# Seven products for eight in three quarters of the second feed-forward matrix

## The chip, the cores and the metric

The kernel runs on one core of a Trainium2 chip. The metric is the device time of one execution in microseconds, the median of several runs. The profile is one execution recorded by the hardware; its times count from the first instruction of the span.

## What is computed

One encoder block on 256 tokens of width 2048 in float32: two gated branches (a chunked gated linear attention and an order-2 Hyena convolution), their merge and output projection, a LayerNorm, a squared-ReLU feed-forward network and a second LayerNorm. The change touches the feed-forward network alone:

```python
h = _layernorm(DEEPNORM_ALPHA * h + mix, ln1_g[l], ln1_b[l])
ff = jnp.square(jax.nn.relu(h @ w_ff1[l])) @ w_ff2[l]      # 2048 -> 8192 -> 2048
h = _layernorm(DEEPNORM_ALPHA * h + ff, ln2_g[l], ln2_b[l])
```

## The kernel before

**Number format.** Every matrix operand is split in two parts: `hi`, the value cast to the matmul's 32-bit format by ScalarE (a copy, line 85), and `lo`, the rest, subtracted by VectorE (line 86, `split_hi_lo`). A product is three matmuls: hi by hi, hi by lo, lo by hi. So each weight that is loaded costs one ScalarE copy and one VectorE subtraction before TensorE can use it.

**Weights.** They come as blocks of 128 partitions by 2048 floats (1 MB), in the order in which they are used. `fetch` (line 93) loads one into one of three `raw` buffers from SyncE's queue (line 99) and splits its two halves of 1024 columns into `whi` and `wlo`, of which there are three buffers each (line 107). `next_block` (line 131) fetches the next block and hands out the oldest one waiting.

**Feed-forward.** The hidden width of 8192 is worked in four quarters of 2048. `ff1(qi)` (line 1073) takes 16 blocks of the first matrix. For a block, `channel_products` (line 140) issues 16 matmuls with 512 columns (line 146: the hi weights against the hi and lo parts of all 256 tokens) and 16 with 256 columns (line 150: the lo weights against the hi part) into one PSUM bank. `channel_sum` (line 155) then copies one half of the bank out with ScalarE (line 158) and adds the other half to it with VectorE (line 159). After two blocks VectorE squares (line 1078) and the result is split into the quarter's activations. `ff2(qi)` (line 1101) takes 16 blocks of the second matrix, four for each group of 512 output columns: `token_products` (line 194) issues for each of four 128-row tiles and each of two 128-token blocks three matmuls with 512 columns (lines 205 to 207), 24 to a block. `add_ff` (line 1089) adds the two banks of a group to the running sum `z1` (line 1094; line 1092 in the first quarter).

The order of the stages is written out: `ff1(0)`, the load of the second LayerNorm's rows, `ff1(1)`, `ff2(0)`, `ff1(2)`, `ff2(1)`, `ff1(3)`, `ff2(2)`, then `ff2(3)` with its last group handled apart so that the final LayerNorm can begin early.

**What sets the order within an engine.** Every engine executes its own instructions in order. The order is fixed when the program is built, by a planner of the framework that follows the order of the code, marked priorities (`tc.high_priority`) and its own estimate of when operands are ready; semaphores then hold an instruction until its operands and its output buffer are free. There are eight PSUM banks, four under the name `mm` and four under `sd`; in the feed-forward stage only `mm` banks are used. GpSimd does nothing in this stage.

Of the kernel before, what the change touches and what calls it, by code (L numbers as in the profile page):

```python
# [16 lines left out]
P = 128  # L17
D = 2048
# [9 lines left out]
CW = D // NCH  # L28
QT = 4
W_OUT_END = 177  # L30
OPENING = 5
PIECES = tuple((k, 1) for k in range(6)) + tuple((k, 2) for k in range(6, KT, 2))

# [9 lines left out]
def block_kernel(  # L43
# [49 lines left out]
    def fetch():  # L93
        n = fetched[0]
        if n >= stop_at[0]:
            return
        fetched[0] = n + 1
        raw = wp.tile([P, D], F32, tag="raw", bufs=3, name=f"raw{n}")
        nc.sync.dma_start(raw, wblk[n])
        parts = []  # L100
        for h in range(2):
            hi, lo = weight_half(n, h)
            split_hi_lo(hi, lo, raw[:, h * 1024:(h + 1) * 1024])
            parts.append((hi, lo))
        queue.append(parts)
# [25 lines left out]
    def next_block():  # L131
        fetch()
        return queue.popleft()
# [3 lines left out]
    def channel_psum(name):  # L137
        return psum_main(name).rearrange("p (a b) -> p a b", a=2)

    def channel_products(ps, act, half, kts, ts=FULL, opens=True):  # L140
        hi, lo = half
        at = [(kt, slice(kt % 8 * P, (kt % 8 + 1) * P)) for kt in kts]

        def high():
            for kt, js in at:
                MM(ps[:, :, ts], hi[:, js], act[:, kt, :, ts], start=(kt == 0 and opens), stop=(kt == KT - 1))  # L146

        def low():
            for kt, js in at:
                MM(ps[:, 0, ts], lo[:, js], act[:, kt, 0, ts], start=False, stop=False)  # L150

        for part in (high, low) if kts[0] == 0 else (low, high):
            part()
# [4 lines left out]
            nc.scalar.activation(low, ps[:, 1], AF.Copy, scale=scale)  # L158
            nc.vector.scalar_tensor_tensor(dst, ps[:, 0], scale, low, op0=ALU.mult, op1=ALU.add)  # L159

    def channel_pair(act, name, dst=None, scale=1.0, begun=None):
        if dst is None:
            dst = base.tile([P, 2, L], F32, tag="sum", name=f"{name}_s")
        for c in range(2):
            if begun:
                ps, parts, n = begun.pop(0)
                finish_block(ps, act, parts, n)
            else:
                ps = channel_psum(f"{name}_{c}")
                parts = next_block()  # L170
                for h in range(2):
                    channel_products(ps, act, parts[h], range(8 * h, 8 * h + 8))
            channel_sum(dst[:, c], ps, f"{name}_l{c}", scale)
            pump()
        return dst

    def high_by_tokens(ps, act, half, kts, ts):
        for kt in kts:
# [55 lines left out]
    def act_tile(pool, tag, name):  # L234
        return pool.tile([P, KT, 2, L], F32R, tag=tag, name=name)
# [679 lines left out]

    tc.keep_in_program_order(nc.scalar.preload_act_table_set("natural_log_exp_and_others"))

    def resident(slots):
        parts = []
        for hi, lo in slots:  # L920
# [4 lines left out]
            for h in range(2):  # L925
                cs = slice(h * 1024, (h + 1) * 1024)
                split_hi_lo(hi[:, cs], lo[:, cs], raw[:, cs])
            parts.append([(hi[:, 0:1024], lo[:, 0:1024]), (hi[:, 1024:], lo[:, 1024:])])
        return parts

    def halves(pool, tag, name):
        t = pool.tile([P, 4, D], F32R, tag=tag, name=name)
# [100 lines left out]
            turn(at, n)  # L1033


    fts = {}

    def begin_three():
        blocks = [queue.popleft(), [], []]
        hx, lx = (ep.tile([P, D], F32R, tag=t, name=f"{t}_f") for t in ("xh", "xl"))  # L1040
# [29 lines left out]
        fetch()  # L1070
        return begun

    def ff1(qi):
        begun = begin_three() if qi == 0 else []
        f = act_tile(ep, "f", f"f{qi}") if qi % 2 == 0 else act_tile(base, "xT", f"f{qi}")
        for c2 in range(8):
            r = channel_pair(hT, f"f{qi}_{c2}", begun=begun)
            sq = nc.vector.scalar_tensor_tensor(r, r, 0.0, r, op0=ALU.max, op1=ALU.mult)
            s = slice(2 * c2, 2 * c2 + 2)
            split_hi_lo(f[:, s, 0], f[:, s, 1], r)  # L1080
            if qi == 0 and 2 <= c2 < 6:
# [3 lines left out]
        fts[qi] = f  # L1085

    st2 = ep.tile([P, NT, 8, 6], F32, tag="bst", bufs=2, name="bst2")

    def add_ff(ps, tb, at, n, qi, last=False):
        zc = z1[:, tb, at:at + n]  # L1090
        if qi == 0:
            nc.vector.scalar_tensor_tensor(zc, zc, ALPHA, ps, op0=ALU.mult, op1=ALU.add)
        else:
            nc.vector.tensor_tensor(zc, zc, ps, op=ALU.add)
        if qi == QT - 1:
            for i in range(n // 256):
                nc.vector.bn_stats(st2[:, tb, at // 256 + i, :], zc[:, i * 256:(i + 1) * 256])
            if not last:
                nc.vector.tensor_tensor(zc, zc, rows2[:, 0, at:at + n], op=ALU.mult)

    def ff2(qi, groups=4):
        for g in range(groups):
            pss = token_group(fts[qi], f"w2_{qi}{g}")
            for tb in range(NT):
                add_ff(pss[tb], tb, g * 512, 512, qi)
# [10 lines left out]
    ff2(3, 3)  # L1116
    parts = resident(halves(ep, "f", "wr2") + halves(ep, "hT", "wr3"))
    minus = ep.tile([P, P], F32, tag="minus", name="minus")
    nc.vector.tensor_scalar(minus, ident, -1.0, None, op0=ALU.mult)
    unit = ep.tile([P, P], F32R, tag="unit", name="unit")  # L1120
    nc.scalar.copy(unit, ident)
    zg = tuple(ep.tile([P, D], F32R, tag=t, name=f"{t}_z") for t in ("xh", "xl"))
    for at in (0, 768):
        split_hi_lo(zg[0][:, at:at + 768], zg[1][:, at:at + 768], z1[:, 1, at:at + 768])

    def affine(tb, at, n, rs, nb):
        zc = z1[:, tb, at:at + n]
# [8 lines left out]
    token_products([ps], fts[3], parts, [0], 0)  # L1136
    pss = [psum_main(f"w2_33_1{ch}") for ch in range(2)]
    add_ff(ps, 0, 1536, 512, 3)
# [4 lines left out]
    column_products([None, pss], fts[3], parts, [1], 0)  # L1143
    CENTRED = ((0, 512), (512, 512), (1024, 256), (1280, 256))
    po = {}
    for at, n in CENTRED[:3]:
        po[at] = psum_side(f"lo{at}")
        for part in zg:
            tc.keep_in_program_order(MM(po[at], unit, part[:, at:at + 512], start=(part is zg[0]), stop=False))
    po[1280] = po[1024][:, 256:]  # L1150
    add_ff(pss[0][:, 0:256], 1, 1536, 256, 3, last=True)
    late = z1[:, 1, 1536:2048]
    with tc.high_priority(), tc.issue_after(done.ins):
        add_ff(pss[1][:, 0:256], 1, 1792, 256, 3, last=True)
# [12 lines left out]
        nc.vector.tensor_tensor(rs, y, t, op=ALU.mult)  # L1167
# [8 lines left out]
def _layout(a):  # L1176
# [24 lines left out]
    for i in range(NCH // 2):  # L1201
# [1 line left out]
    f1 = chan(a["w_ff1"][0])  # L1203
    w2 = a["w_ff2"][0]
    f1q = [f1[16 * i:16 * (i + 1)] for i in range(QT)]
    f2q = [tok(w2[D * i:D * (i + 1)]) for i in range(QT)]
# [105 lines left out]
```

## Time and profile before

| what | value |
|---|---|
| median of 3 runs | 1826.8 us (1826.16 to 1826.92) |
| span of the profiled execution | 1826.2 us |
| TensorE busy | 1817.0 us, granted clock 1.000 |
| VectorE, ScalarE, GpSimd busy | 1286.8, 924.1 and 80.4 us |
| bytes moved | 399.55 MB, 219 GB/s in the mean |

The profiled execution's time is its span, 1826.2 us; the three runs lie within 0.7 us of it. In the views, PE is TensorE's matmuls, PEld its loads of the stationary operand, DVE is VectorE, ACT ScalarE, POOL GpSimd and SP SyncE. Matmuls are pipelined, so the duration of one (its own start to its own end) is longer than the time by which the stream advances. A row of a group gives: line, engine, operation, output and inputs with their shapes, count, then the total busy time, the mean duration in ns, and the idle time of that engine ahead of these instructions with what ended it.

### The profile page before, as it was taken

The page shows a single profiled execution, that of the slowest core. Times are in us where ns is not written, and L with a number is a line of the kernel's source. Part 1 is how long each engine was busy: PE and PEld are TensorE (multiplying, and loading weights), DVE is VectorE, ACT ScalarE, POOL GpSimd, SP SyncE. Part 2 cuts the span into 40 slices and gives each one's busy share as a digit, 9 for nine tenths or more (in the row PEclk, how much of TensorE's full clock was granted, in tenths as well). Part 3 has the DMA queues.
Part 4 walks back from the last instruction along what each step waited for, and adds up shares of the span by engine and source line. Part 5 has one row for each costly group of instructions (what it writes and reads, how often), then busy time and mean ns, then how long its engine had stood idle before and what let it go on. Part 6 is the DMA issues. An engine that isn't in the chain of part 4 may idle for free.

```text
span 1826.2 us, 22887 instructions
## 1 busy us (share of the span) xinstructions
PE 1817.0 (99%) x8931; PEld 1533.8 (84%) x8931; DVE 1286.8 (70%) x1587; ACT 924.1 (51%) x1207; POOL 80.4 (4%) x121
## 2 busy tenths in 40 slices
PE   9999999999999999999999999999999999999998
PEld 7888888888888888888888889888888888888887
DVE  6789887875689899898755567666545655565467
ACT  6678668865444444444544445444434443443332
POOL 1011110000111101020000000000000000000000
PEclk9999999999999999999999999999999999999999
DMA  8668765345788979796544763545554555555453
GB/s 326 222 257 293 253 220 204 141 162 210 235 281 255 320 249 274 259 281 230 215 186 185 288 252 137 210 185 188 193 196 186 193 195 187 195 195 187 188 197 123
DMA packets 65452, 399.55 MB, mean 219 GB/s; under 512 B 8280, under 2 KB 10856, under 8 KB 24640
## 3 DMA queue, kind: packets, MB, share of 16 engines
q1 hardware_dynamic: 47808, 336.61, 49.1%
q0 software_dynamic: 10480, 41.81, 9.9%
q10 hardware_dynamic: 7056, 19.67, 3.0%
q8 instruction: 70, 1.15, 0.2%
q14 instruction: 38, 0.31, 0.0%
HBM read 369.28 MB, written 16.25 MB: 211 GB/s over the span
## 4 chain that ended last, share of the span: by engine, by line
PE 97%; DMA 1%; DVE 1%; ACT 0%; issue 0%; SPq 0%; DVEq 0%; POOL 0%; ACTq 0%
PE f L146 12%; PE f L150 6%; PE w L205 6%; PE w L207 6%; PE w L206 6%; PE g L206 3%; PE g L205 3%; PE g L207 3%; PE ux L207 3%; PE ux L206 3%; PE ux L205 3%; PE k L146 2%; PE v L206 2%; PE v L205 2%; PE v L207 2%; PE go L206 2%
## 5 line engine op out<-in xcount | busy, mean ns | idle before, releaser
L86 DVE TENSOR_TENSOR wlo<-raw,whi 128x1024 fp32r<-128x1024 f32 x584 | 712.3, 1222 | 356.5 <-ACT whi L85 353.4
L85 ACT CAST whi<-raw 128x1024 fp32r<-128x1024 f32 x584 | 614.0, 1053 | 576.1 <-PE w L207 186.5
L146 PE MATMUL f<-hT,whi 128*128 128x512 f32 x984 | 235.1, 391 | 0.0
L146 PEld LDWEIGHTS f<-hT,whi 128*128 128x128 f32 x984 | 180.8, 188 | 35.0
L206 PE MATMUL w<-wlo,f 128*128 128x512 f32 x480 | 186.7, 389 | 0.0
L207 PE MATMUL w<-whi,f 128*128 128x512 f32 x480 | 186.7, 389 | 0.0
L205 PE MATMUL w<-whi,f 128*128 128x512 f32 x480 | 167.4, 389 | 0.0
L150 PEld LDWEIGHTS f<-hT,wlo 128*128 128x128 f32 x984 | 126.2, 191 | 4.8
L150 PE MATMUL f<-hT,wlo 128*128 128x256 f32 x984 | 127.7, 283 | 0.0
L158 ACT ACTIVATE f_l<-f 128x256 f32<-128x256 f32 x64 | 24.6, 384 | 162.2 <-PE f L146 159.3
L207 PEld LDWEIGHTS w<-whi,f 128*128 128x128 f32 x480 | 90.1, 188 | 18.8
L205 PEld LDWEIGHTS w<-whi,f 128*128 128x128 f32 x480 | 90.1, 188 | 18.7
L206 PEld LDWEIGHTS w<-wlo,f 128*128 128x128 f32 x480 | 90.1, 188 | 18.7
L159 DVE SCALAR_TENSOR_TENSOR f_s<-f,f_l 128x256 f32<-128x256 f32 x64 | 27.2, 425 | 105.0 <-ACT f_l L158 105.0
L206 PE MATMUL g<-wlo,xT 128*128 128x512 f32 x256 | 100.1, 391 | 0.0
L207 PE MATMUL ux<-whi,xT 128*128 128x512 f32 x256 | 99.9, 390 | 0.0
L207 PE MATMUL g<-whi,xT 128*128 128x512 f32 x256 | 99.8, 390 | 0.0
L206 PE MATMUL ux<-wlo,xT 128*128 128x512 f32 x256 | 99.6, 389 | 0.0
L205 PE MATMUL g<-whi,xT 128*128 128x512 f32 x256 | 93.8, 392 | 0.0
L205 PE MATMUL ux<-whi,xT 128*128 128x512 f32 x256 | 89.7, 389 | 0.0
L206 PEld LDWEIGHTS g<-wlo,xT 128*128 128x128 f32 x256 | 48.1, 188 | 10.1 <-DVE wlo L86 0.2
L206 PEld LDWEIGHTS ux<-wlo,xT 128*128 128x128 f32 x256 | 48.1, 188 | 10.1
(428 smaller groups left out, 3235.4 us busy)
## 6 DMA issues: line engine op xcount, KB each, us to landing
raw<-wblk SPq DMA_DIRECT2D x300, 1024.0 KB, 4.9
Td<-T POOLq DMA_DIRECT2D x32, 384.0 KB, 5.5
conv_sb<-conv_rows SPq DMA_DIRECT2D x12, 1024.0 KB, 11.7
Tl<-Td POOLq DMA_DIRECT2D x16, 768.0 KB, 9.1
w<-w4s ACTq DMA_DIRECT2D x16, 512.0 KB, 5.7
xw<-first SPq DMA_DIRECT2D x5, 896.0 KB, 13.4
zr<-ln_rows ACTq DMA_DIRECT2D x4, 1024.0 KB, 10.5
cx<-shift POOLq DMA_DIRECT2D x8, 508.0 KB, 8.4
```

What stands on the lines that cost most here:

```text
L85: return (nc.scalar.copy(hi, src), nc.vector.tensor_tensor(lo, src, hi.bitcast(F32), op=ALU.subtract))
L86: nc.vector.tensor_tensor(lo, src, hi.bitcast(F32), op=ALU.subtract))
L146: MM(ps[:, :, ts], hi[:, js], act[:, kt, :, ts], start=(kt == 0 and opens), stop=(kt == KT - 1))
L150: MM(ps[:, 0, ts], lo[:, js], act[:, kt, 0, ts], start=False, stop=False)
L158: nc.scalar.activation(low, ps[:, 1], AF.Copy, scale=scale)
L159: nc.vector.scalar_tensor_tensor(dst, ps[:, 0], scale, low, op0=ALU.mult, op1=ALU.add)
L205: MM(pss[tb], sh, wh, start=(kt == 0), stop=False)
L206: MM(pss[tb], sh, wl, start=False, stop=False)
L207: MM(pss[tb], sl, wh, start=False, stop=(kt == KT - 1))
```

## The change

Three of the four quarters of the second matrix are multiplied by Strassen's scheme (in the form with shared sums). Two 128-row tiles by 1024 columns of the second matrix make a 2 by 2 array of 128x512 pieces, and two token blocks by the same two tiles of the activations make a 2 by 2 array of 128x128 pieces. Instead of eight products of such pieces there are seven, each still three matmuls with 512 columns, so 21 matmuls to a block of 1 MB instead of 24. The price is sums: four sums of the weights' pieces and four of the activations' pieces before, and sums of the seven results behind.

- `fetch_sums` replaces `fetch` for the blocks of the second matrix in three quarters. It loads the block, splits the first 1024 columns and the last 512 as they are, and has **GpSimd** make four sums of 512 columns (one instruction of 1024 columns and two of 512, each reading two tiles), which ScalarE and VectorE then split as two halves of 1024. So 3584 columns of each block are split where 2048 were. The sums' tile (tag `xh`) and the tiles of the split sums (`whx`, `wlx`) exist once.
- `forms` makes the four sums of the activations on GpSimd (four instructions of 128 columns) and splits 384 and 512 columns; in the third phase, for the last quarter, which stays as it was, it splits 512 plain columns.
- `ff_phase(q)` replaces `ff2(q)` and `ff1(q + 1)`. It alternates one block of the second matrix (`forms_products`, 21 matmuls) with one of the first (32 matmuls), 16 of each. The output is worked in two groups of 1024 columns, of eight blocks each. The seven results of a group hold seven PSUM banks, so one bank is left for the first matrix.
- `take_sums` empties the seven banks after eight blocks, into `z1` or into `zacc`, which takes the place of the LayerNorm rows; four of them are ScalarE copies in the first phase, all others VectorE adds. `join_sums` makes the final sums: the first group's beside the second half of the third phase, seven on GpSimd and one on VectorE; the second group's on VectorE behind the third phase. The second LayerNorm's rows are loaded after that.
- The last quarter and the final LayerNorm do the same work as before, with their tiles in other places. The order of the weights in memory follows the new order of use.

```diff
+        if FF_PAIRS <= n < FF_PAIRS + 96 and (n - FF_PAIRS) % 2 == 0:
+            queue.append(fetch_sums(n))
+            return
...
+    def quad_sum(i, c, ps, name):
+        low = base.tile([P, L], F32, tag="low", name=name)
+        dst = quads(i)[:, 2 * c:2 * c + 2][:, ::-1]
+        halves = [a.rearrange("p (t j) -> p t j", j=P) for a in (ps[:, 0], low)]
+        with tc.high_priority():
+            nc.scalar.copy(low, ps[:, 1])
+            nc.vector.tensor_tensor(dst, halves[0], halves[1], op=ALU.add)
+
+    def forms(i, plain=False):
+        q, slot = quads(i), fa_slot(i)
+        if plain:
+            split_hi_lo(slot[:, 0, 0:4], slot[:, 1, 0:4], q)
+            return
+        split_hi_lo(slot[:, 0, 0:3], slot[:, 1, 0:3], q[:, 1:4])
+        t = ep.tile([P, 4, P], F32, tag="aff", bufs=1, name=f"fw{i}")
+        TT = nc.gpsimd.tensor_tensor
+        TT(t[:, 0], q[:, 0], q[:, 2], op=ALU.subtract)
+        TT(t[:, 1], q[:, 1], t[:, 0], op=ALU.subtract)
+        TT(t[:, 2], q[:, 3], t[:, 1], op=ALU.subtract)
+        TT(t[:, 3], q[:, 0], q[:, 1], op=ALU.subtract)
+        split_hi_lo(slot[:, 0, 3:7], slot[:, 1, 3:7], t)
...
+    def fetch_sums(n):
+        if not whx:
+            whx[0] = ep.tile([P, D], F32R, tag="xl", name="whx")
+            wlx[0] = ep.tile([P, D], F32R, tag="wlx", name="wlx")
+        raw = wp.tile([P, D], F32, tag="raw", bufs=3, name=f"raw{n}")
+        nc.sync.dma_start(raw, wblk[n])
+        s = ep.tile([P, D], F32, tag="xh", name=f"ws{n}")
+        u = [raw[:, k * 512:(k + 1) * 512] for k in range(4)]
+        v = [s[:, k * 512:(k + 1) * 512] for k in range(4)]
+        hi, lo = weight_half(n, 0)
+        split_hi_lo(hi, lo, raw[:, 0:1024])
+        fa_slot(4)
+        at = 7168 + n // 2 % 2 * 512
+        h1, l1 = (t[:, at:at + 512] for t in fa)
+        split_hi_lo(h1, l1, u[3])
+        TT = nc.gpsimd.tensor_tensor
+        TT(s[:, 0:1024].rearrange("p (a b) -> p a b", a=2), raw[:, 0:1024].rearrange("p (a b) -> p a b", a=2),
+           u[2].rearrange("p (a b) -> p a b", a=1).broadcast_to([P, 2, 512]), op=ALU.add)
+        TT(v[2], v[0], u[1], op=ALU.add)
+        TT(v[3], v[2], u[3], op=ALU.add)
+        for k in range(2):
+            cs = slice(k * 1024, (k + 1) * 1024)
+            split_hi_lo(whx[0][:, cs], wlx[0][:, cs], s[:, cs])
...
+    def forms_products(pss, parts, i):
+        slot = fa_slot(i)
+        for ps, (wh, wl, f) in zip(pss, parts):
+            sh, sl = slot[:, 0, f], slot[:, 1, f]
+            MM(ps, sh, wh, start=(i == 0), stop=False)
+            MM(ps, sh, wl, start=False, stop=False)
+            MM(ps, sl, wh, start=False, stop=(i == 7))
...
+    def ff_phase(q):
+        joins = []
+        for k in range(16):
+            g, i = divmod(k, 8)
+            if i == 0:
+                pss = [psum_side(f"w{q}{g}{j}") if j < 4 else psum_main(f"w{q}{g}{j}") for j in range(7)]
+            forms_products(pss, next_block(), i)
+            if i == 7:
+                take_sums(q, g, pss)
+                if q == 2 and g == 0:
+                    joins = join_sums(0, nc.gpsimd.tensor_tensor)
+            if g:
+                if i < 7:
+                    forms(i, q == 2)
+                if joins:
+                    joins.pop(0)()
+            ps = channel_psum(f"f{q + 1}_{k}")
+            parts = next_block()
+            for h in range(2):
+                channel_products(ps, hT, parts[h], range(8 * h, 8 * h + 8))
+            quad_sum(k // 2, k % 2, ps, f"f{q + 1}_l{k}")
+            if k % 2:
+                squares(k // 2)
+        forms(7, q == 2)
+        if q == 2:
+            for j in joins + join_sums(1, nc.vector.tensor_tensor):
+                j()
...
-    ff1(0)
+    ff1_first()
+    for q in range(3):
+        ff_phase(q)
     rows2 = load_rows(2)
-    ff1(1)
-    ff2(0)
-    ff1(2)
-    ff2(1)
-    ff1(3)
-    ff2(2)
...
-        + [f1q[0], f1q[1], f2q[0], f1q[2], f2q[1], f1q[3], f2q[2], f2q[3]], axis=0)
+        + [f1q[0]] + pairs + [tok(w2[3 * D:])], axis=0)
```

More of the change, by code (lines that the diff above doesn't have):

```diff
@@ L159, in channel_sum, with channel_pair @@
             nc.vector.scalar_tensor_tensor(dst, ps[:, 0], scale, low, op0=ALU.mult, op1=ALU.add)
-    def channel_pair(act, name, dst=None, scale=1.0, begun=None):
-        if dst is None:
-            dst = base.tile([P, 2, L], F32, tag="sum", name=f"{name}_s")
+    def channel_pair(act, name, dst, scale=1.0):
         for c in range(2):
[L165 to L172, printed above, removed]
+            ps = channel_psum(f"{name}_{c}")
+            parts = next_block()
+            for h in range(2):
+                channel_products(ps, act, parts[h], range(8 * h, 8 * h + 8))
             channel_sum(dst[:, c], ps, f"{name}_l{c}", scale)
             pump()
-        return dst
     def high_by_tokens(ps, act, half, kts, ts):
@@ L916, in block_kernel, with resident_pieces @@
     tc.keep_in_program_order(nc.scalar.preload_act_table_set("natural_log_exp_and_others"))
-    def resident(slots):
-        parts = []
-        for hi, lo in slots:
+    def resident_pieces(parts):
+        for part in parts:
             n = fetched[0]
@@ L924, in resident @@
             nc.sync.dma_start(raw, wblk[n])
[L925 to L928, printed above, removed]
-        return parts
+            for h, (hi, lo) in enumerate(part):
+                split_hi_lo(hi, lo, raw[:, h * 1024:(h + 1) * 1024])
+        return parts
+    def resident(slots):
+        return resident_pieces([[(hi[:, c:c + 1024], lo[:, c:c + 1024]) for c in (0, 1024)] for hi, lo in slots])
     def halves(pool, tag, name):
@@ L1071, in begin_three @@
         return begun
-    def ff1(qi):
-        begun = begin_three() if qi == 0 else []
-        f = act_tile(ep, "f", f"f{qi}") if qi % 2 == 0 else act_tile(base, "xT", f"f{qi}")
-        for c2 in range(8):
[L1077 to L1081, printed above, removed]
+    zacc = zr[:, 2:4].rearrange("p a (b c) -> p (a b) c", c=512).rearrange("p (n k) c -> p n k c", n=2)
@@ new lines, in block_kernel, with fa_slot, quads @@
+    fa = [base.tile([P, 8192], F32R, tag="xT", name="fa0"), None]
+    def fa_slot(i):
+        if fa[1] is None:
+            fa[1] = ep.tile([P, 8192], F32R, tag="f", name="fa1")
+        t = fa[i // 4][:, i % 4 * 1792:(i % 4 + 1) * 1792]
+        return t.rearrange("p (h k j) -> p h k j", h=2, j=P)
+    quad_tiles = [ep.tile([P, 4, P], F32, tag="fr", bufs=3, name=f"fr{i}") for i in range(3)]
+    quad_tiles.append(base.tile([P, 4, P], F32, tag="sum", name="fr3"))
+    def quads(i):
+        return quad_tiles[i % 4]
@@ new lines, in block_kernel, with __getitem__, ff1_first @@
+    class Quarter:
+        def __getitem__(self, at):
+            _, kt, part, ts = at
+            return fa_slot(kt // 2)[:, part, ((1, 0), (3, 2))[kt % 2][ts.start // P]]
+    def ff1_first():
+        begun = begin_three()
+        for c2 in range(8):
+            for c in range(2):
+                if begun:
+                    ps, parts, n = begun.pop(0)
+                    finish_block(ps, hT, parts, n)
+                else:
+                    ps = channel_psum(f"f0_{c2}_{c}")
+                    parts = next_block()
+                    for h in range(2):
+                        channel_products(ps, hT, parts[h], range(8 * h, 8 * h + 8))
+                quad_sum(c2, c, ps, f"f0_{c2}_l{c}")
+            sq = squares(c2)
+            forms(c2)
+            if 2 <= c2 < 6:
@@ new lines, in forms_products, with take_sums @@
+    def forms_products(pss, parts, i):
[5 more added lines that the diff above has]
+            MM(ps, sl, wh, start=False, stop=(i == 7))
+    def take_sums(q, g, pss):
+        c1, c2 = slice(g * 1024, g * 1024 + 512), slice(g * 1024 + 512, g * 1024 + 1024)
+        STT, TT = nc.vector.scalar_tensor_tensor, nc.vector.tensor_tensor
+        dst = [zacc[:, g, 0], z1[:, 0, c2], z1[:, 0, c1], zacc[:, g, 1], zacc[:, g, 2], zacc[:, g, 3], z1[:, 1, c1]]
+        for k, (d, ps) in enumerate(zip(dst, pss)):
+            with tc.high_priority():
+                if k in (1, 2, 6):
+                    if q == 0:
+                        STT(d, d, ALPHA, ps, op0=ALU.mult, op1=ALU.add)
+                    else:
+                        TT(d, d, ps, op=ALU.add)
+                elif q == 0:
+                    nc.scalar.copy(d, ps)
+                else:
+                    TT(d, d, ps, op=ALU.add)
@@ new lines, in join_sums @@
+    def join_sums(g, TT):
+        c1, c2 = slice(g * 1024, g * 1024 + 512), slice(g * 1024 + 512, g * 1024 + 1024)
+        p1, p5, p7, p6 = (zacc[:, g, k] for k in range(4))
+        z11, z12, z21, z22 = z1[:, 0, c1], z1[:, 0, c2], z1[:, 1, c1], z1[:, 1, c2]
+        return [
+            lambda: TT(z11, z11, p1, op=ALU.add),
+            lambda: TT(p6, p6, p1, op=ALU.subtract),
+            lambda: TT(z12, z12, p6, op=ALU.add),
+            lambda: TT(z12, z12, p5, op=ALU.add),
+            lambda: TT(p6, p6, p7, op=ALU.add),
+            lambda: TT(z21, z21, p6, op=ALU.subtract),
+            lambda: TT(p6, p6, p5, op=ALU.add),
+            lambda: nc.vector.scalar_tensor_tensor(z22, z22, ALPHA, p6, op0=ALU.mult, op1=ALU.add),
+        ]
@@ new lines, in ff_phase @@
+    def ff_phase(q):
[15 more added lines that the diff above has]
+            ps = channel_psum(f"f{q + 1}_{k}")
+            parts = next_block()
+            for h in range(2):
+                channel_products(ps, hT, parts[h], range(8 * h, 8 * h + 8))
+            quad_sum(k // 2, k % 2, ps, f"f{q + 1}_l{k}")
[5 more added lines that the diff above has]
+                j()
@@ L1087, in block_kernel, with add_ff @@
     st2 = ep.tile([P, NT, 8, 6], F32, tag="bst", bufs=2, name="bst2")
-    def add_ff(ps, tb, at, n, qi, last=False):
+    def add_ff(ps, tb, at, n, last=False):
         zc = z1[:, tb, at:at + n]
[L1091 to L1105, printed above, removed]
-    ff1(0)
-    rows2 = load_rows(2)
-    ff1(1)
-    ff2(0)
-    ff1(2)
-    ff2(1)
-    ff1(3)
-    ff2(2)
-    stop_at[0] = nblk - 4
-    ff2(3, 3)
-    parts = resident(halves(ep, "f", "wr2") + halves(ep, "hT", "wr3"))
+        nc.vector.tensor_tensor(zc, zc, ps, op=ALU.add)
+        for i in range(n // 256):
+            nc.vector.bn_stats(st2[:, tb, at // 256 + i, :], zc[:, i * 256:(i + 1) * 256])
@@ new lines, in add_ff, with quarters @@
+        if not last:
+            nc.vector.tensor_tensor(zc, zc, rows2[:, 0, at:at + n], op=ALU.mult)
+    ff1_first()
+    for q in range(3):
+        ff_phase(q)
+    rows2 = load_rows(2)
+    f3 = Quarter()
+    stop_at[0] = nblk - 4
+    for g in range(3):
+        pss = token_group(f3, f"w2_3{g}")
+        for tb in range(NT):
+            add_ff(pss[tb], tb, g * 512, 512)
+    def quarters(*tiles):
+        at = [t[:, k:k + 1024] for t in tiles for k in range(0, t.shape[1], 1024)]
+        return [[(at[0], at[1]), (at[2], at[3])], [(at[4], at[5]), (at[6], at[7])]]
@@ L1118, in block_kernel @@
+    spare = [t[:, 7168:8192] for t in fa]
+    own = [ep.tile([P, D], F32R, tag=t, name=f"{t}_r") for t in ("xh", "xl", "wlx")]
+    parts = resident_pieces(quarters(*own, *spare)
+                            + [[(a[:, c:c + 1024], b[:, c:c + 1024]) for c in (0, 1024)] for a, b in halves(ep, "hT", "wr3")])
     minus = ep.tile([P, P], F32, tag="minus", name="minus")
     nc.vector.tensor_scalar(minus, ident, -1.0, None, op0=ALU.mult)
-    unit = ep.tile([P, P], F32R, tag="unit", name="unit")
+    unit = base.tile([P, 4, P], F32R, tag="dfth", name="unit")[:, 0]
@@ L1121, in block_kernel @@
     nc.scalar.copy(unit, ident)
-    zg = tuple(ep.tile([P, D], F32R, tag=t, name=f"{t}_z") for t in ("xh", "xl"))
-    for at in (0, 768):
-        split_hi_lo(zg[0][:, at:at + 768], zg[1][:, at:at + 768], z1[:, 1, at:at + 768])
+    zg = [weight_half("z", h) for h in range(2)]
+    for h, n in ((0, 1024), (1, 512)):
+        split_hi_lo(zg[h][0][:, 0:n], zg[h][1][:, 0:n], z1[:, 1, h * 1024:h * 1024 + n])
     def affine(tb, at, n, rs, nb):
@@ L1147, in block_kernel @@
         po[at] = psum_side(f"lo{at}")
-        for part in zg:
-            tc.keep_in_program_order(MM(po[at], unit, part[:, at:at + 512], start=(part is zg[0]), stop=False))
+        for part in range(2):
+            z = zg[at // 1024][part][:, at % 1024:at % 1024 + 512]
+            tc.keep_in_program_order(MM(po[at], unit, z, start=(part == 0), stop=False))
     po[1280] = po[1024][:, 256:]
-    add_ff(pss[0][:, 0:256], 1, 1536, 256, 3, last=True)
+    add_ff(pss[0][:, 0:256], 1, 1536, 256, last=True)
     late = z1[:, 1, 1536:2048]
     with tc.high_priority(), tc.issue_after(done.ins):
-        add_ff(pss[1][:, 0:256], 1, 1792, 256, 3, last=True)
+        add_ff(pss[1][:, 0:256], 1, 1792, 256, last=True)
         mv = ep.tile([P, 2], F32, tag="mv", bufs=2, name="mvl")
@@ L1205, in _layout @@
     f1q = [f1[16 * i:16 * (i + 1)] for i in range(QT)]
-    f2q = [tok(w2[D * i:D * (i + 1)]) for i in range(QT)]
+    quad = w2[:3 * D].reshape(3, 8, 2, P, 2, 2, 512)
+    quad = np.stack([quad[:, :, 0, :, :, 0], quad[:, :, 1, :, :, 1], quad[:, :, 0, :, :, 1], quad[:, :, 1, :, :, 0]],
+                    axis=3)
+    quad = quad.transpose(0, 4, 1, 2, 3, 5).reshape(3, 16, P, D)
+    pairs = [np.stack([quad[i], f1q[i + 1]], axis=1).reshape(32, P, D) for i in range(3)]
     g1, g2 = tok(seg["g"][:, :D]), tok(seg["g"][:, D:])
```

19 lines of the change are left out of this document (14 added, 5 removed).

## The prediction, made before the result was known

> **What bounds the kernel now.** I read the page's busy times first, then the slices and the chain, then the feed-forward stage alone.
>
> ```profile
> span 1826.2 us, 22887 instructions
> PE 1817.0 (99%) x8931; PEld 1533.8 (84%) x8931; DVE 1286.8 (70%) x1587; ACT 924.1 (51%) x1207; POOL 80.4 (4%) x121
> PE   9999999999999999999999999999999999999998
> POOL 1011110000111101020000000000000000000000
> PE 97%; DMA 1%; DVE 1%; ACT 0%; issue 0%; SPq 0%; DVEq 0%; POOL 0%; ACTq 0%
> ```
>
> TensorE is busy 99% of the span and is 97% of the chain of waits, so a matmul taken away is time taken away, as long as nobody else becomes late. GpSimd is empty in the second half, where the feed-forward stage lies. Next the busy times by stage; each row is a stretch, its length, then PE, PEld, DVE, ACT and POOL:
>
> ```profile
> core 0: us, PE busy (x) PEld busy (x) DVE busy (x) ACT busy (x) POOL busy (x), PEclk, DMA share, GB/s
> 1289.06:1376.10 87.04, 87.04 (x386) 72.07 (x385) 44.79 (x42) 34.65 (x34) 0.00 (x0) 1.00 0.51 193
> 1376.10:1465.17 89.07, 89.07 (x514) 78.71 (x513) 54.25 (x63) 41.42 (x54) 0.00 (x0) 1.00 0.51 191
> 1465.17:1552.21 87.04, 87.04 (x385) 72.07 (x385) 44.80 (x42) 34.64 (x34) 0.00 (x0) 1.00 0.51 192
> 1552.21:1641.28 89.07, 89.07 (x513) 78.72 (x513) 54.23 (x63) 41.35 (x54) 0.00 (x0) 1.00 0.51 191
> ```
>
> The rows are second matrix, first matrix, second, first. A quarter of the second is 16 blocks of 24 matmuls, 384 in 87.04 us: **0.2267 us** a matmul, without a gap. A quarter of the first is 16 blocks in 89.07 us: **5.567 us** a block. VectorE is busy 99.0 of these 176.1 us.
>
> ```profile
> DVE wlo L86 <- ACT whi L85: 353.4, 331, 3.0
> ACT whi L85 <- PE w L207: 186.5, 115, 1.7
> ```
>
> VectorE waits for ScalarE and ScalarE for matmuls to free a buffer: the splitting runs ahead and is held back by TensorE. There is slack, and the question is how much of it the new sums use up.
>
> **TensorE.** Three quarters go from 384 to 336 matmuls: 3 x 48 x 0.2267 = 32.6 us less. A pair (one block of each matrix) is 21 x 0.2267 + 5.567 = 10.33 us instead of 11.01; 48 pairs are 495.7 instead of 528.3 us.
>
> **VectorE and ScalarE.** The durations:
>
> ```profile
> L86 DVE TENSOR_TENSOR wlo<-raw,whi 128x1024 fp32r<-128x1024 f32 x584 | 712.3, 1222 | 356.5 <-ACT whi L85 353.4
> L85 ACT CAST whi<-raw 128x1024 fp32r<-128x1024 f32 x584 | 614.0, 1053 | 576.1 <-PE w L207 186.5
> L86 DVE TENSOR_TENSOR f<-f_s,f 128x512 fp32r<-128x512 f32 x29 | 19.9, 685 | 0.0
> L159 DVE SCALAR_TENSOR_TENSOR f_s<-f,f_l 128x256 f32<-128x256 f32 x64 | 27.2, 425 | 105.0 <-ACT f_l L158 105.0
> L1078 DVE SCALAR_TENSOR_TENSOR f_s<-f_s 128x512 f32<-128x512 f32 x29 | 20.1, 692 | 1.0
> L1094 DVE TENSOR_TENSOR zr<-zr,w 128x512 f32<-128x512 f32 x23 | 14.8, 681 | 1.0 <-PE w L207 1.0
> L618 DVE TENSOR_TENSOR qx<-qi,e 128x128 f32<-128x128 f32 x8 | 2.2, 280 | 0.0
> ```
>
> A pair splits five halves of 1024 and one of 512 (before: four of 1024): 5 x 1.222 + 0.685 = 6.80 us; one add of the bank's halves, 0.425; half a squaring, 0.346: 7.57 us. A phase of 16 pairs is 121.1. The eight sets of forms add 0.685 and, for 384 columns (between 0.280 and 0.685, by length 0.55), 1.24 us each: 9.9, or 5.5 us in the third phase. Emptying banks is 6 x 0.681 = 4.1 us in the first phase and 14 x 0.681 = 9.5 in the others. The phases come to 135.1, 140.5 and 136.1: **412 us** of VectorE beside 495.7 of TensorE. ScalarE does 5.5 copies of 1.053 us and little else in a pair, well below.
>
> **GpSimd.** No row has GpSimd compute; all its 80.4 us are DMA issues and four memsets. I bound it by VectorE's rows.
>
> ```profile
> L569 DVE TENSOR_TENSOR_SCAN gb<-scan_sb,gm 128x256 f32<-128x256 f32 x8 | 5.1, 678 | 0.1
> L472 POOL DMA_DIRECT2D Td<-T x32 | 19.3, 607 | 214.4 <-DVE T L468 214.0 <-issue 0.4
> ```
>
> From 685 and 1222 ns, a VectorE add is 1.05 ns an element and 0.15 us fixed: a pair's three instructions with 2048 elements would be 2.6 us. The slowest row per element is the scan, (678 - 150) / 256 = 2.07 ns, which would give 4.7 us. A program on general cores that takes in two operands an element is nearer to the scan, and I take **4.7**. At that rate the four forms are 1.65 us and a join of 512 columns 1.21. Phases one and two: 16 x 4.7 + 8 x 1.65 = 88.4 each; three: 75.2 + 7 x 1.21 = 83.7. Together 260 us, or 5.4 a pair; at VectorE's rate 148 us. The Trainium skill (GPSIMD Engine Reference, section Elementwise — side-by-side cycle accounting) gives 4497 ns for an add of 2048 floats; no run here shows it yet, and the sum would be about the same by it.
>
> **Does GpSimd run beside VectorE?** This decides the case, and the trace before has no answer, since nothing of GpSimd's reads tiles beside VectorE. The bounds are all of it hidden and none of it. Alone, neither engine passes TensorE. End to end they are 412 + 260 = 672 us, 14.0 a pair. I take the serial end, on two grounds. First, the sums' tile exists once: GpSimd cannot begin block k+1 before both splits of block k's sums are done, and these cannot begin before GpSimd is. The loop is 4.7 + 1.05 + 2 x 1.22 = 8.2 us and four hand-overs, and through it VectorE must carry in order 5.1 us of other work a pair, 6.4 in the second half of a phase, nearly all of which must fall into the 4.7 us of GpSimd to be free. Second, both engines stream two operands out of the same memory at the same time, where the trace shows only one of them ever doing so. What waits: behind a VectorE split of the sums stand the splits of the first matrix, and the add that frees the one PSUM bank left to that matrix; TensorE stands behind both.
>
> So the 528.3 us become 672: **+144 us**. The Trainium skill (SBUF — State Buffer, section Who interferes with whom) says that a VectorE instruction with two SBUF inputs and a GpSimd instruction that reads SBUF exclude each other, the later blocking until the first has finished. By that rule the splits stand against the sums, while the 48 adds of bank halves and 34 emptyings, which read PSUM, do not; the sum would be 44 us lower, near 1927, before any idle gap. By the trace alone, in which the subtractions keep their length, nothing need stretch:
>
> ```profile
> L86 DVE TENSOR_TENSOR wlo<-raw,whi x584: 1198/1225/1229, 27.8 to 1788.3; 128x1024 fp32r<-128x1024 f32 x195
> ```
>
> That is with GpSimd issuing DMAs or idle, which proves little for one that computes.
>
> **The other parts** I cost at nothing. In the first quarter VectorE has 4 x 1.222 + 2 x 0.425 + 0.692 + 1.24 = 7.7 us for two blocks (8.4 with a row add) and GpSimd 1.65, in series 10.0 under TensorE's 11.1; the excess would cost if that were passed. The last quarter and the end keep their counts. Behind phase three come eight VectorE adds (5.5 us) and then the LayerNorm rows:
>
> ```profile
> zr<-ln_rows ACTq DMA_DIRECT2D x4, 1024.0 KB, 10.5
> raw<-wblk SPq DMA_DIRECT2D x300, 1024.0 KB, 4.9
> ```
>
> They are wanted only after four blocks of 5.44 us, so 5.5 + 10.5 lie under 21.8 us; without that cover, up to 5 us. SyncE's loads stay at 2 MB a pair and 4.9 us each; a raw buffer is now held until GpSimd has read it, but three buffers serve two loads in 14 us.
>
> Could TensorE's waiting lower its clock? At the end, where it stands idle, the profile shows this:
>
> ```profile
> 1820.00:1824.00 4.00, 1.09 (x3) 0.19 (x1) 1.78 (x4) 0.00 (x0) 0.00 (x0) 1.00 0.82 262
> 1824.00:1827.00 3.00, 0.00 (x0) 0.00 (x0) 0.00 (x0) 0.00 (x0) 0.00 (x0) 0.78 0.02 3
> ```
>
> The clock read 0.78 only in a stretch with no matmul at all. Waits here are 14.0 - 10.3 = 3.7 us a pair, in pieces. A clock of 0.78 would make a pair's matmuls 13.2 us, still under 14.0, so I add nothing and keep it for the upper end.
>
> **Forecast: 1826.8 + 144 = 1971 us.** The profiled span, 1826.2, lies 0.6 below the median of the runs; the difference carries over. Its own range: from 1890 (a cheaper GpSimd, the PSUM reads hidden) to 2060 (VectorE also waits out one ScalarE copy of 1.05 us in each pair, +50, and some clock).
>
> **Rivals.**
> - *Free overlap, faster.* GpSimd's sums run wholly beside VectorE, and the order of VectorE's queue fits. For it: 8.2 is under 10.33, GpSimd is otherwise empty, VectorE at 412 of 495.7 us (83%) still fits. Against it: in the second half of a phase VectorE has 8 x 7.57 + 9.9 + 4.8 = 75.3 of 82.6 us, 91%, and in-order waits must cost no more than 0.9 us a pair. Price: 1826.8 - 32.6 = 1794, and some 6 us at the six changes of group, where seven banks (4.8 us of VectorE) must be emptied within one block of 5.57: **1800**. It decides from the point where the pair falls under 11.0 us, that is when over 3.0 of GpSimd's 5.4 us a pair are hidden.
> - *Half hidden, slightly slower.* Half of GpSimd's 260 us lies beside VectorE: 412 + 130 = 542, **+14, 1841**. The same region is reached if GpSimd is serial but as quick as VectorE: 412 + 148 = 560, +32, 1858.
> - *No change.* Savings and stalls cancel within 0.2% (3.7 us), which is about what a measurement of this kernel can tell from no change: only by accident.
>
> **Chances.** No row shows the two engines computing together, so these are judgements on the terms above. The serial end needs one condition, that the sums and the splits do not overlap, and it is slower even with GpSimd at its cheap end (1858). The free case needs three: GpSimd no slower than the scan, VectorE undisturbed by it, and a queue order that keeps a 91% loaded engine within 0.9 us of its waits. Serial 0.72; half hidden 0.09; free 0.17; no change 0.02. So slower 0.81, faster 0.17. The range of 8 in 10 takes in the serial and half-hidden cases, 1830 to 2060, and leaves out the free case.
>
> **What would show it.** In the phases: a pair every 14 us instead of 11.0; TensorE near 74% busy there at clock 1.00; a GpSimd add of 1024 columns near 2.3 us; VectorE's subtractions stretched beyond 1229 ns, or gaps before them ended by GpSimd and ScalarE; ScalarE waiting for GpSimd instead of for matmuls. If instead TensorE stays above 95% busy with pairs of 10.3 to 10.6 us while GpSimd and VectorE are busy in the same microseconds, my serial term is wrong. If GpSimd's add of 1024 columns takes 1.2 us, its price is.

## The result, and the profile after

The changed kernel takes **1895.18 us** (median of 4 runs, 1894.37 to 1896.74) against 1826.86 us before: a ratio of 1.0375, 95% interval 1.0361 to 1.0390. It is slower by 68 us, where 144 were forecast: the direction was right, one of the two grounds for it held, and the forecast loss was twice too large.

The page of the changed kernel, the lines that answer to those of before:

```profile
span 1892.6 us, 23147 instructions
PE 1819.7 (96%) x8787; PEld 1516.6 (80%) x8787; DVE 1583.8 (84%) x1726; ACT 1002.1 (53%) x1335; POOL 508.9 (27%) x368
PE   9999999999999999999999999899889988988998
DVE  6798878775789898988465677899999999999967
POOL 1010100000101111110000003666876587566300
PE 68%; DVE 18%; DMA 5%; POOL 4%; issue 3%; ACT 1%; DVEq 0%; ACTq 0%; POOLq 0%
```

TensorE's share of the chain fell from 97% to 68%, and VectorE and GpSimd came into it. Where GpSimd is busiest, VectorE's slices read 9, and TensorE's fall to 8 in places. The three phases by half (first group of outputs, second group, three times), then the rest of the span; the columns are those of the stretches shown before:

```profile
1195.63:1294.94 99.31, 89.76 (x443) 74.22 (x441) 93.82 (x69) 53.51 (x67) 62.97 (x35) 0.98 0.49 179
1294.94:1402.09 107.15, 93.07 (x425) 74.59 (x424) 105.27 (x81) 55.55 (x75) 81.76 (x49) 0.94 0.45 166
1402.09:1493.10 91.01, 85.43 (x426) 70.51 (x424) 87.34 (x66) 47.00 (x57) 57.05 (x32) 1.00 0.46 171
1493.10:1600.54 107.44, 91.32 (x426) 74.20 (x424) 106.94 (x84) 53.26 (x71) 81.83 (x48) 0.95 0.45 164
1600.54:1694.42 93.88, 86.67 (x426) 71.87 (x424) 89.24 (x67) 47.49 (x58) 55.83 (x29) 0.98 0.46 170
1694.42:1794.80 100.38, 87.75 (x425) 71.61 (x424) 99.19 (x78) 48.04 (x60) 58.13 (x27) 0.98 0.50 183
1794.80:1892.60 97.80, 92.11 (x445) 76.55 (x444) 70.73 (x100) 34.87 (x39) 0.00 (x0) 0.99 0.48 172
```

The phases take 599.2 us, where the same work took 528.3 before (the 599.2 include some 2.8 us of the first quarter's last block); VectorE is busy for 581.8 of them, 97%. In the second half of phases one and two, where the activation sums are added, it is busy 98% and over 99%. What follows the phases takes 97.8 us, as before (1826.2 - 1728.3). So all of the loss lies in the phases, and there VectorE is the bound. Its groups between 1190 and 1760 us say why:

```profile
L87 DVE TENSOR_TENSOR wlo<-raw,whi 128x1024 fp32r<-128x1024 f32 x138 | 242.3, 1778 | 1.1 <-ACT whi L86 1.1
L87 DVE TENSOR_TENSOR fa<-raw,fa 128x512 fp32r<-128x512 f32 x45 | 93.5, 2077 | 10.6 <-ACT fa L86 10.6
L1096 DVE SCALAR_TENSOR_TENSOR fr<-fr 128x512 f32<-128x512 f32 x24 | 41.6, 1732 | 0.7
L1092 DVE TENSOR_TENSOR fr<-f,f_l 128x256 f32<-128x256 f32 x47 | 19.3, 410 | 0.0
L1193 DVE TENSOR_TENSOR zr<-zr,w 128x512 f32<-128x512 f32 x12 | 7.9, 673 | 0.0
```

The instructions that read two operands from SBUF are stretched (1222 to 1778 ns, 685 to 2077, 692 to 1732); the two that read one operand from PSUM keep their length (425 and 681 before, 410 and 673 now). One stretch of the timeline shows the hand-over; start and duration in us, first VectorE, then GpSimd:

```profile
1296.10 1.22 DVE L87 TENSOR_TENSOR wlo<-raw,whi 128x1024 fp32r<-128x1024 f32 x1
1297.24 2.90 DVE L87 TENSOR_TENSOR fa<-raw,fa 128x512 fp32r<-128x512 f32 x1
1300.06 0.41 DVE L1092 TENSOR_TENSOR fr<-f,f_l 128x256 f32<-128x256 f32 x1
1300.51 1.33 DVE L1096 SCALAR_TENSOR_TENSOR fr<-fr 128x512 f32<-128x512 f32 x1
```

```profile
1296.26 3.33 POOL L1155 TENSOR_TENSOR ws<-raw 128x1024 f32<-128x1024 f32 x1 [4.04 <-DVE wlx L87]
1299.67 1.62 POOL L1157 TENSOR_TENSOR ws<-ws,raw 128x512 f32<-128x512 f32 x1
1301.37 1.61 POOL L1158 TENSOR_TENSOR ws<-ws,raw 128x512 f32<-128x512 f32 x1
```

VectorE's subtraction of 1024 columns is first and keeps its 1.22 us, to 1297.32. GpSimd's sum, started at 1296.26, ends at 1299.59, 2.27 us after that. VectorE's next subtraction, 0.685 us alone, starts at 1297.24 and ends at 1300.14, 0.55 us after the sum. GpSimd's second sum ends at 1301.29, 1.15 us after that subtraction, while the add out of PSUM (1300.06 to 1300.47) runs through beside it. They take turns, instruction by instruction. (Two VectorE instructions in a row overlap a little, here by 0.08 us.)

### The profile page after: what moved, and what is told of

It is laid out like the page before. It is cut to its first block, busy times and chain, and to the rows that moved or that the text cites. A ratio compares the mean times of both kernels' runs of the same rounds, so it can differ in the third digit from the quotient of the medians.

```text
span 1892.6 us, 23147 instructions
## 1 busy us (share of the span) xinstructions
PE 1819.7 (96%) x8787; PEld 1516.6 (80%) x8787; DVE 1583.8 (84%) x1726; ACT 1002.1 (53%) x1335; POOL 508.9 (27%) x368
## 4 chain that ended last, share of the span: by engine, by line
PE 68%; DVE 18%; DMA 5%; POOL 4%; issue 3%; ACT 1%; DVEq 0%; ACTq 0%; POOLq 0%
DVE wlo L87 7%; DVE fa L87 6%; DMA raw<-wblk 5%; PE g L203 3%; PE g L202 3%; PE g L204 3%; PE ux L204 3%; PE ux L202 3%; PE ux L203 3%; PE f L150 2%; DVE fr L1096 2%; PE r L202 2%; PE r L204 2%; PE r L203 2%; PE k L150 2%
## 5 line engine op out<-in xcount | busy, mean ns | idle before, releaser
L86 ACT CAST whi<-raw 128x1024 fp32r<-128x1024 f32 x536 | 558.6, 1052 | 422.3 <-PE ux L204 88.5
L150 PE MATMUL f<-hT,whi 128*128 128x512 f32 x984 | 255.5, 406 | 12.6 <-DVE fr L1092 12.5
L86 ACT CAST whx<-ws 128x1024 fp32r<-128x1024 f32 x96 | 100.8, 1050 | 152.8 <-POOL ws L1158 95.4
L1155 POOL TENSOR_TENSOR ws<-raw 128x1024 f32<-128x1024 f32 x48 | 134.1, 2793 | 156.8 <-DMA raw<-wblk 103.6
L87 DVE TENSOR_TENSOR wlx<-ws,whx 128x1024 fp32r<-128x1024 f32 x96 | 131.0, 1379 | 0.8
L87 DVE TENSOR_TENSOR fa<-raw,fa 128x512 fp32r<-128x512 f32 (+1 forms) x49 | 101.9, 2080 | 12.5 <-ACT fa L86 12.5
L1106 POOL TENSOR_TENSOR fw<-fr 128x128 f32<-128x128 f32 x24 | 23.1, 964 | 285.8 <-DVE fr L1096 263.0
L1158 POOL TENSOR_TENSOR ws<-ws,raw 128x512 f32<-128x512 f32 x48 | 90.9, 1894 | 3.5
L1157 POOL TENSOR_TENSOR ws<-ws,raw 128x512 f32<-128x512 f32 x48 | 83.2, 1733 | 3.7
L1175 PE MATMUL w<-wlx,fa 128*128 128x512 f32 x192 | 77.0, 401 | 6.9 <-DVE wlx L87 6.9
L86 ACT CAST fa<-raw 128x512 fp32r<-128x512 f32 (+1 forms) x49 | 30.8, 629 | 93.5 <-DMA raw<-wblk 93.5
```

The lines of the kernel that those rows point to most:

```text
L86: return (nc.scalar.copy(hi, src), nc.vector.tensor_tensor(lo, src, hi.bitcast(F32), op=ALU.subtract))
L87: nc.vector.tensor_tensor(lo, src, hi.bitcast(F32), op=ALU.subtract))
L1155: TT(s[:, 0:1024].rearrange("p (a b) -> p a b", a=2), raw[:, 0:1024].rearrange("p (a b) -> p a b", a=2), u[2].rearrange("p (a b) -> p a b" ...
L1157: TT(v[2], v[0], u[1], op=ALU.add)
L1158: TT(v[3], v[2], u[3], op=ALU.add)
L1175: MM(ps, sh, wl, start=False, stop=False)
```

## The experiments

The theory: a GpSimd sum and a VectorE instruction with two SBUF operands exclude each other. Rival A: the chain through the one sums tile. Rival B: VectorE has too many splits, and GpSimd does not matter.

**No weight sums** (e1). The sums are left out and the block's own columns split in their place:

```diff
-        TT(s[:, 0:1024]..., raw[:, 0:1024]..., u[2]..., op=ALU.add)
-        TT(v[2], v[0], u[1], op=ALU.add)
-        TT(v[3], v[2], u[3], op=ALU.add)
...
-            split_hi_lo(whx[0][:, cs], wlx[0][:, cs], s[:, cs])
+            split_hi_lo(whx[0][:, cs], wlx[0][:, cs], raw[:, cs])
```

> Leaves out the four weight sums: ScalarE and VectorE split the block's own 2048 columns in their place, as many instructions of the same shapes as in the changed kernel; GpSimd makes only the activation sums. Theory (GpSimd and a VectorE instruction with two SBUF inputs exclude each other): the phases fall from 599 us to TensorE's 496 us or a little more, so 1795 to 1810 us, and VectorE's subtractions return to about 1222 ns. Rival A (the chain through the one sums tile: GpSimd, then ScalarE, then VectorE, in series): also near 1800. Rival B (VectorE has simply too many splits, GpSimd does not matter): stays above 1870.

Measured 1795.96 us, ratio to the kernel before 0.9831 (0.9815 to 0.9847). TensorE is the bound again, here in a stretch that holds all the phases:

```profile
1195.60:1700.00 504.40, 504.10 (x2582) 430.88 (x2581) 411.25 (x445) 312.76 (x387) 92.50 (x77) 1.00 0.58 207
```

Its subtractions, as a group, are back near their length:

```profile
L87 DVE TENSOR_TENSOR wlo<-raw,whi 128x1024 fp32r<-128x1024 f32 x157 | 193.8, 1256 | 41.3 <-ACT whi L86 41.2
```

Rival B falls: with every split in place VectorE is busy for 411 of 504 us and holds nobody up. The whole loss, 99 us from here, hangs on the weight sums.

**Sums that nobody reads** (e2). GpSimd makes the sums, and the splits read the block itself, by the last two lines of the diff above alone.

> GpSimd makes the same weight sums from the same tiles, but nothing reads them: the splits read the block's own columns, so no instruction of VectorE or ScalarE waits for a sum. Leaves out the use of the sums. Theory (exclusion): the subtractions stay stretched to 1400 to 1800 ns and the time stays between 1865 and 1900 us. Rival A (chain through the sums): near 1800, subtractions at 1222 ns. Rival B (too many splits): stays above 1870, but with subtractions at 1222 ns.

Measured 1902.49 us, 1.0413 (1.0398 to 1.0429), a little slower than the changed kernel and 2 us past my range, and the subtractions are stretched:

```profile
L87 DVE TENSOR_TENSOR wlo<-raw,whi 128x1024 fp32r<-128x1024 f32 x126 | 217.4, 1747 | 2.5 <-ACT whi L86 2.5
```

No instruction waits for a sum here. Rival A falls.

**Fills in place of the sums** (e3). The chain through the tile stays; GpSimd only writes:

```diff
-        TT(...)  # the three sums
+        for a in (0, 512, 1024, 1536):
+            for _ in range(3):
+                nc.gpsimd.memset(s[:, a:a + 512], 0.25)
```

> In place of the weight sums GpSimd fills the sums tile with a constant, three times over (twelve fills of 512 columns a block, so that it is busy for some microseconds), and the splits read that tile as before: the chain through the one tile stays, but GpSimd reads nothing beside VectorE. Leaves out the sums. Theory (exclusion of reads): 1795 to 1820 us with subtractions near 1222 ns. Rival A (chain): 1860 to 1900 us if the fills take as long as the sums, 4.7 us or more. A third outcome, subtractions stretched although GpSimd only writes, would say that the exclusion holds for writes as well.

Measured 1805.12 us, 0.9884 (0.9869 to 0.9898). Its groups:

```profile
L87 DVE TENSOR_TENSOR wlo<-raw,whi 128x1024 fp32r<-128x1024 f32 x152 | 188.3, 1259 | 36.2 <-ACT whi L86 36.1
L1155 POOL MEMSET ws<- 128x512 f32 x552 | 261.2, 526 | 126.9 <-DVE wlx L87 126.9
```

Twelve fills keep GpSimd busy for about 5.7 us a block (261.2 / 46), longer than the 4.9 us that the sums need alone, and VectorE is not held up. So a GpSimd that only writes does not exclude VectorE. What is left as the cause of the stretch is that GpSimd reads; every reading instruction here has two operands, so what one with a single operand does is not shown. The run is 9 us over e1, which I put down to the chain, with a longer link than the real one; no run parts it from the fills themselves.

One more thing differs in e1 and e3: GpSimd no longer holds the block's `raw` buffer, so loads can start earlier. Late loads are not the loss: they would leave VectorE idle, and in the changed kernel it is idle for 17 of the 599 us, while its subtractions are stretched.

**The sums on VectorE** (e4), `nc.vector` for `nc.gpsimd` in `fetch_sums`:

> The same weight sums on VectorE: one add of 1024 and two of 512 columns a block, 2.6 us at the measured rate, and nothing of them on GpSimd; the activation sums stay there. Theory (exclusion): VectorE's own work in the phases grows from 412 to 538 us and GpSimd's falls to the 40 us or so of the activation sums and joins, so phases of 545 to 575 us and 1840 to 1870 us: faster than the changed kernel although VectorE does more, but not faster than the kernel before. Rival B (VectorE has too much to do and GpSimd's part is free): slower than the changed kernel, 599 + 126, near 2020 us.

Measured 1829.38 us, 1.0016 (1.0006 to 1.0025): 0.2% over the kernel before, 66 us under the changed one, and 11 us under the range of 1840 to 1870 that I gave. The stretch that holds most of the phases, and the row of the sum of 1024 columns, now VectorE's:

```profile
1195.60:1700.00 504.40, 486.46 (x2418) 406.38 (x2417) 479.40 (x544) 291.61 (x365) 121.10 (x79) 0.98 0.53 192
L1155 DVE TENSOR_TENSOR ws<-raw 128x1024 f32<-128x1024 f32 x48 | 60.3, 1257 | 1.5 <-DMA raw<-wblk 1.2
```

VectorE does more and is done sooner. Rival B fell again.

**The activation sums on VectorE** (e5), the same edit in `forms` alone:

> Only the activation sums move from GpSimd to VectorE (four instructions of 128 columns, 0.28 us each alone); the weight sums stay on GpSimd. Theory (exclusion, priced by the hand-overs of the changed kernel's trace, where GpSimd holds VectorE for 0.32 us an instruction of 128 columns, 1.28 us a set): 16 sets in the phases give back 20 us of blocking and take some 9 to 18 us of VectorE, so 1880 to 1895 us. Rival B (VectorE's own load decides): slower than the changed kernel by 16 x 4 x 0.28 = 18 us, near 1913.

Measured 1887.98 us, 1.0337 (1.0323 to 1.0351), 7 us under the changed kernel: as the theory priced it.

**One weight sum twice** (e6):

```diff
+        TT(s[:, 0:1024]..., raw[:, 0:1024]..., u[2]..., op=ALU.add)
         TT(s[:, 0:1024]..., raw[:, 0:1024]..., u[2]..., op=ALU.add)
```

> GpSimd makes its 1024-column sum twice, with the same operands and the same result. Theory (exclusion, priced by the hand-overs: a blocked 1024-column sum ends 2.26 us after the VectorE instruction before it): 48 x 2.26 = 108 us more where VectorE has no idle time left, so near 2003 us, 1980 to 2010. Rival C (a part of GpSimd's time is hidden, 38% as the changed kernel's 170 us of stretch for 275 us of sums would suggest): 48 x 2.36 x 0.62 = 70 us more, near 1965.

Measured 2012.94 us, 1.1023 (1.1008 to 1.1038): 118 us over the changed kernel, 2.45 us for each added sum, and 3 us past the upper end of my range. That is a little over the 2.26 us of a hand-over and far from the 70 of rival C: in time, an added microsecond of GpSimd is paid in full. But the time does not come the way that I said, by VectorE having no idle time left. VectorE's rows between 1190 and 1760 us:

```profile
L87 DVE TENSOR_TENSOR wlo<-raw,whi 128x1024 fp32r<-128x1024 f32 x118 | 230.5, 1961 | 49.4 <-ACT whi L86 49.2
L87 DVE TENSOR_TENSOR wlx<-ws,whx 128x1024 fp32r<-128x1024 f32 x76 | 111.0, 1468 | 30.0 <-ACT whx L86 29.8
```

Ahead of these it waits 79 us for ScalarE's copies, where the changed kernel had 2, and GpSimd's first sum of a block waits 106 us in all for VectorE's split of the sums before, against 42. So with longer sums the chain through the one tile comes in beside the exclusion, and how the 118 us divide between them is open.

**VectorE relieved** (g1, g2). From e4, in the phases:

```diff
-                    MM(ps[:, :, ts], hi[:, js], act[:, kt, :, ts], ...)
+                    for i in range(2):
+                        MM(ps, hi[:, js], hT[:, kt, i], ...)   # ps: 256 columns
...
-            quad_sum(k // 2, k % 2, ps, f"f{q + 1}_l{k}")
+            nc.scalar.activation(quads(k // 2)[...], ps..., AF.Relu)
             if k % 2:
-                squares(k // 2)
+                nc.scalar.activation(quads(k // 2), quads(k // 2), AF.Square)
```

> The weight sums on VectorE as in e4, and VectorE relieved: in the phases the hi weights' products with both parts of the tokens go into the same 256 columns (twice 16 matmuls of 256 columns instead of 16 of 512, +0.17 us a block by the 119 ns of such a matmul), so no add of the bank's halves is left, and ScalarE does the rectifying out of PSUM and the squaring. VectorE loses 48 x 0.425 + 24 x 0.69 = 37 us of about 538, TensorE gains 8 on 496. Theory: phases of 505 to 525 us, 1803 to 1822 us, faster than both kernels. Rival: the saved VectorE time is taken up by waits in its queue or by ScalarE: 1826 or more.

Measured 1819.04 us, 0.9961 (0.9949 to 0.9974): 0.4% under the kernel before, so faster than both kernels; its rival, 1826 or more, falls. g2 adds this in `forms`:

```diff
-        TT = nc.gpsimd.tensor_tensor
-        TT(t[:, 0], q[:, 0], q[:, 2], op=ALU.subtract)
+        TT = nc.vector.tensor_tensor
+        TT(t[:, 0::3], q[:, 0:1].broadcast_to([P, 2, P]), q[:, 2:0:-1], op=ALU.subtract)
...
-        TT(t[:, 3], q[:, 0], q[:, 1], op=ALU.subtract)
```

> As g1, and the activation sums on VectorE as three instructions (0.42 + 2 x 0.28 us a set) instead of four on GpSimd (4 x 0.32 us of exclusion a set): nothing of GpSimd is left beside VectorE but seven final adds. Theory: 3 to 10 us less than g1. Rival: the same as g1 within 3 us, if GpSimd's short sums fall in VectorE's idle time.

Measured 1818.24 us, **0.9953** (0.9939 to 0.9967). The 0.8 us from g1 are no gain that the runs can tell, so here its rival held. g2's page:

```profile
span 1816.5 us, 24501 instructions
PE 1799.7 (99%) x9555; PEld 1546.7 (85%) x9555; DVE 1488.7 (82%) x1870; ACT 1020.7 (56%) x1359; POOL 94.3 (5%) x128
PE 96%; DVE 2%; DMA 1%; ACT 0%; issue 0%; DVEq 0%; SPq 0%; ACTq 0%
```

With nothing but seven final adds on GpSimd, TensorE is the bound again, and some of the saved matmuls are saved. In g1 it was busy for 99% of the span as well, so the step that counts is the one from e4 to g1.

## Why the prediction was right or wrong

**TensorE, 32.6 us less:** right. Without the weight sums (e1) the kernel is 30.6 us under the one before. Of the 6 us that I gave the changes of group, about 2 came.

**VectorE's own work, 412 us; GpSimd's price, 4.7 us a pair:** right. VectorE is busy 411 us in e1's stretch of 504, which is all the phases and a few us more. On GpSimd the shortest sums of each shape in the changed kernel are these (shortest, median and longest, in ns):

```profile
L1158 POOL TENSOR_TENSOR ws<-ws,raw x48: 1285/2130/2266, 1194.4 to 1779.5; 128x512 f32<-128x512 f32 x48
L1155 POOL TENSOR_TENSOR ws<-raw x48: 2375/2725/3452, 1187.0 to 1775.3; 128x1024 f32<-128x1024 f32 x48
```

If the shortest are those that nothing held up, a pair alone is 2.38 + 2 x 1.29 = 4.9 us, and the scan was a good neighbour.

**The serial end, "End to end they are 412 + 260 = 672 us":** this is the step that failed, by its size. The phases took 599 us, 12.5 a pair and not 14.0, with TensorE busy for 534 of them (89%) where I had named 74%. The engines exclude each other, but I added whole durations of everything they do. What excludes is less, as the hand-overs show. Of VectorE's 412 us, the adds out of PSUM (44 us, which the text itself set aside as a lower sum) run beside GpSimd. Of every other instruction the start does not count: a blocked subtraction ends 0.55 us after GpSimd, not 0.685, and one of 1024 columns 1.08 us after it, not 1.22 (1.08 or 1.09 in 115 of the trace's 122 such cases; in the other seven the sum ended within 0.07 us of the subtraction's start). The start of one lies beside the end of the other. GpSimd's instructions likewise end 2.26, 1.15 and 0.32 us after VectorE for 1024, 512 and 128 columns. The sum in these prices: GpSimd 48 x (2.26 + 2 x 1.15) + 64 x 0.32 + 7 x 1.15 = 247 us; VectorE 240 x 1.08 + 96 x 0.55 + 16 x 0.41 (the forms' 384 columns) = 319 us. Together **566 us**, and 599 were measured; the other 33 are VectorE's idle time (17) and turns at which the next one was not ready. The sum in these prices, and that last split, are worked out and not tried by themselves.

**The grounds for the serial end:** one of two held. The chain through the one sums tile was the wrong ground for this kernel: e2 is slow without it and e3 fast with it. (It shows once GpSimd's part is longer still, in e6.) The second, that both stream operands from SBUF at the same time, was the right one. The rule of the Trainium skill (SBUF — State Buffer, section Who interferes with whom) agrees with these traces in each part: a VectorE instruction with two SBUF inputs and a GpSimd instruction that reads SBUF take turns (1222 to 1778 ns), one with an input from PSUM does not wait (410 ns), and a GpSimd that only writes does not hold VectorE up (1259 ns in e3). By it I had 1927 us before idle gaps, still 32 too many, since it too was worked with whole durations.

**Clock:** I added nothing for it, as the waits come in pieces. It did fall, to 0.94 and 0.95 in the second halves of phases one and two, and the mean duration of a matmul of the first matrix rose there (the row is of the second half of phase one):

```profile
L150 PE MATMUL f<-hT,whi 128*128 128x512 f32 x129 | 36.9, 433 | 3.2 <-DVE fr L1092 3.1
```

That was 391 ns before. What it cost is not shown by itself; VectorE, busy for 97% of the phases, was the bound.

**The rest:** nothing at the end and nothing in the first quarter, as costed. Of the rivals, free overlap failed at the named condition, VectorE undisturbed. "Half hidden", 1841 to 1858, came nearer in its number than in its mechanism: VectorE lost 170 us (582 - 412) to the 260 that I had for GpSimd, two thirds of them, and by the prices above what was hidden lay in the PSUM reads and the starts. That its number lies nearer is luck.

## What to carry to other kernels

Before work is moved from a loaded VectorE to an idle GpSimd, look at where VectorE's operands come from: if both are in SBUF, GpSimd's sums take their time from VectorE (here 2.26 us held for a sum that VectorE makes itself in 1.26 in e4), and the idle engine was no cover at all. Price such a pair as one resource, by the time that each holds it (here 1.08 and 2.26 us for 1024 columns), and leave out what reads PSUM. A scheme that trades matmuls for sums paid here only as far as VectorE had time: the sums had to move to VectorE, and other work away from it, to turn a loss of 3.8% into a gain of 0.5%.

## What the runs showed of the hardware that was not expected

The exclusion goes instruction by instruction, but it leaves out the first 0.13 to 0.14 us of a VectorE instruction: the blocked one ends 1.08 instead of 1.22 us after the release. Fills on GpSimd (526 ns for 512 columns in the mean) leave VectorE alone. TensorE's granted clock came down to 0.94 over a stretch of 107 us in which it was busy for 93, and further in e6, whose stretch from 1195.6 us reads:

```profile
1195.60:1700.00 504.40, 411.71 (x1785) 317.49 (x1784) 413.99 (x310) 218.92 (x281) 380.35 (x205) 0.90 0.38 140
```

That is a clock of 0.90 with TensorE busy for 412 of 504 us, so it does not take a long stretch without matmuls. Two stretches of the changed kernel, one behind the other, show one such fall:

```profile
1327.90:1331.30 3.40, 1.57 (x11) 1.48 (x12) 3.40 (x2) 1.47 (x4) 2.85 (x2) 0.99 0.15 29
1331.30:1334.70 3.40, 3.40 (x10) 2.64 (x9) 3.40 (x5) 1.72 (x3) 0.98 (x2) 0.50 0.94 395
```

TensorE is busy for 1.57 of 3.40 us, and in the next 3.40 us, in which it is busy throughout, the clock is at half.
